# The middle 1024 columns of both mixers' output projections as a pair of column blocks on eight PSUM banks, three of its eight couples by seven products

## The chip, the core and the metric

One NeuronCore of a Trainium2 chip runs the whole program in one launch. TensorE (PE) multiplies into PSUM, eight banks of 512 float32 columns on 128 partitions; VectorE (DVE), ScalarE (ACT) and GpSimd (POOL) do the elementwise work; SyncE (SP) issues the weight transfers. Each engine works through its own queue in order and waits on semaphores of the others. The metric is device time in microseconds, the median of several runs. Before the change it is 2400.95 us (2400.9 to 2401.26, three runs).

## What is computed

The reference is a two-layer encoder trunk on 256 tokens of width 2048, in float32. A layer is a norm, a token mixer with a residual add, a second norm and a gated feed-forward with a residual add. Layer 0 mixes with an mLSTM, layer 1 with an HGRN2; both end in an output projection `y @ w_out`, 256 x 2048 times 2048 x 2048, which is what the change touches.

```python
for layer in range(DEPTH):
    hn = rmsnorm(h, norm_mix_g[layer])
    if layer % N_MIXERS == 0:
        mix = mlstm_mixer(hn, ...)      # ends in  y @ w_out
    else:
        mix = hgrn_mixer(hn, ...)       # ends in  y @ w_out
    h = h + mix
    h = h + conv_glu(rmsnorm(h, norm_ffn_g[layer]), w_up, conv_w, conv_b, w_down)
return rmsnorm(h, final_g)
```

## The kernel before

**Precision.** A float32 product is made of three matmuls in a faster type (`F32R`). Each operand is split into a high part, which is the value rounded to that type, and a low part, which is the rest; then hi x hi, hi x lo and lo x hi are added in PSUM. For weights the split is done while the kernel runs: `parts` (L130) copies 1024 columns of `raw` to `wh` on ACT (L133) and subtracts on DVE, `wl = raw - wh` (L134). Activations are split once, by `split` (L325), into tiles of 128 features whose first 256 columns are the high part of all tokens and whose last 256 are the low part.

**The stream.** The program is a list of `Chunk`s, run by `stream` (L258). Each chunk reads its weights through one common sequence of pieces: `load_raw` (L123) brings 2048 columns into one of three `raw` buffers, and `parts` turns these into pieces of 1024 columns in rings of four `wh` and four `wl` tiles (`WB`). `fetch` keeps `LOOK` = 3 pieces ahead of PE. There are three kinds of chunk. "fm" makes 128 features x 256 tokens with the weights as the stationary operand (L304, L308). "tm" makes 256 tokens x 512 columns in two PSUM banks with the activations as the stationary operand (L320), 16 tiles x 2 token halves x 3 matmuls = 96 matmuls. "st" makes 256 tokens x 1024 columns, a pair of column blocks, in all eight banks (`squares_by_seven`, L204).

**A couple by seven.** In "st" two activation tiles and two column blocks form a couple: with token halves and tiles it is a 2 x 2 block matrix A times a 2 x 2 block matrix B, 8 products of 3 matmuls, 24 matmuls of 128 x 512. For the couples in `ch.seven` a scheme after Strassen and Winograd makes it with 7 products, 21 matmuls. It needs sums of the blocks of B (`combine`, L178: T1 to T4, one of them from `raw` in a 1024-wide subtraction, L184, two in 512-wide ones, L186 and L187, then split into `th` by ACT, L189, and `tl` by DVE, L190) and sums of the blocks of A (`token_sums`, L1003, into a tile `sx` with high and low part). Four of the seven products belong to more than one of the four results. They are gathered in four banks of their own, P1, P6, P7 and P5 (pool `psm`), while the other three go straight to the four result banks C11, C12, C21 and C22 (pool `psa`). After the last couple by seven `mid` (L1021) adds the four shared banks to the residual `hm` through `u2` and `u3`: a copy on ACT, five 512-wide adds on DVE and three on POOL (L1030 to L1032). After the last couple `done` adds the result banks (L1037). Before the change this serves the first parts of the feed-forward's down projection, with `SEVEN` = couples 1, 3, 5 and 7 of eleven.

**Output projections.** Before the change, each mixer's output projection is four "tm" chunks of 512 columns from `project` (L480). When a block is done, two DVE adds put it into `hm` (L486), and `norm.add(c)` (L367) sums its squares on ACT and queues `turn` (L372), which transposes the four new 128-feature tiles on PE through a bank of pool `psa` (L379) and splits them into the next stage's activations `xt` (L326, L327). Side work of that sort waits in the list `side`, which is stepped between matmuls. The next stage's first up run needs all sixteen `xt` tiles.

**Order.** The code names an order, and the framework's list scheduler then reorders instructions within each engine by its own cost estimates, as the program is built; only instructions wrapped in `pin` keep theirs. What is said below about positions in a queue was read from the built programs.

**Names.** `ya` and `yb` are the output projections' activations in the mLSTM and the HGRN. `mm` are tiles of the four `psm` banks, `pc` and `pz` tiles of the four `psa` banks. `LEAD` is an unused tile that shifts what follows it in SBUF. `idle` (L1096) are matmuls on ones that PE makes while the first weights load.

Of the kernel before, what the change touches and what calls it, by code (L numbers as in the profile page):

```python
# [15 lines left out]
P = 128  # L16
T = 256
# [30 lines left out]
SEVEN = (1, 3, 5, 7)  # L48

# [7 lines left out]
def trunk_kernel(ctx, tc, xT, x_d, fg_d, pp_d, cst_d, w_gate, w_first, w_aq, w_ak, w_av, w_ao, w_aout,  # L57
                 w_bq, w_bv, w_bg, w_bout, w_up, w_d0, w_d1, w_d2, out, mscr):
# [53 lines left out]
    side = Side()  # L112
# [56 lines left out]
    def split_squares(ch, parts):  # L169
# [23 lines left out]
        for u in range(units):  # L193
            r = raw(u)
            if u + 1 in ch.seven:
                combine(u + 1)
            wh, wl = parts(r[:, 0:1024], 1024)
            yield wh, wl, 1
            if 2 * u + 1 < ch.nk:
                m = 512 if u in ch.seven else 1024  # L200
                wh, wl = parts(r[:, 1024:1024 + m], m)
                yield wh, wl, sums.pop(u, None)

    def squares_by_seven(ch, fetch, ready):  # L204
# [4 lines left out]
        begun = set()  # L209

# [13 lines left out]
        for u in range(units):  # L224
# [120 lines left out]
    class Norm:  # L345
# [26 lines left out]
        def turn(self, c):  # L372
            yield 2.5
            for k0 in (4 * c, 4 * c + 2):
                pz = aux("pz")
                for k in (k0, k0 + 1):
                    for t in range(2):
                        o = (k - k0) * T + t * P
                        pe.transpose(pz[:, o:o + P], hm[:, t, k * P:(k + 1) * P], ident)  # L379
                for k in (k0, k0 + 1):  # L380
                    self.take(k, pz[:, (k - k0) * T:(k - k0 + 1) * T])
                yield 1.0
            if c == 3:
                self.total()
                self.finish()
                self.spread()
# [108 lines left out]
    def slot(j, name, more=None):  # L495
        where = keep if j < KT else more
        return where.tile([P, 2 * T], F32R, tag=f"yt{j}", name=f"{name}{j}")


    def mlstm(norm, nxt):  # L500
# [273 lines left out]
        def end():  # L774
            side.drain()
            stack.close()

        tail = project(lambda c: w_aout[c], KT, yx, nxt)
        tail[1].before = end
        return chunks + tail  # L780


    def hgrn(norm, nxt):
# [197 lines left out]
        def end():  # L981
            side.drain()
            stack.close()

        tail = project(lambda c: w_bout[c], KT, yx, nxt)
        tail[1].before = end
        return chunks + tail


    def ffn(layer, norm, nxt):  # L990
# [11 lines left out]

        def token_sums(u, a, b, S, SX):  # L1003

            sx = box["mp"].tile([P, 1024], F32R, tag=f"sx{SEVEN.index(u)}", name="sx")
            for i, (x, y, op) in enumerate(((a[:, P:T], b[:, P:T], ALU.add), (a[:, P:T], a[:, 0:P], ALU.subtract),
                                            (S[:, 0:P], a[:, 0:P], ALU.subtract), (b[:, 0:P], S[:, 2 * P:3 * P], ALU.subtract))):
                dve.tensor_tensor(S[:, i * P:(i + 1) * P], x, y, op)
            act.copy(sx[:, 0:512], S)
            dve.tensor_tensor(sx[:, 512:1024], S, sx[:, 0:512].bitcast(F32), ALU.subtract)  # L1010
            SX[u] = sx

        def pair(src, nk, q, GT, SX, norm):

            u = []

            def part(t, c):
                o = 1024 * q + 512 * c
                return hm[:, t, o:o + 512]

            def mid(ps):  # L1021
                P1, P6, P7, P5 = ps
                u2, u3 = (box["mp"].tile([P, 512], F32, tag=n, name=n) for n in ("u2", "u3"))
                act.copy(u2, P1)
                dve.tensor_tensor(part(0, 0), part(0, 0), P1, ALU.add)
                dve.tensor_tensor(u2, u2, P6, ALU.add)
                dve.tensor_tensor(u3, u2, P7, ALU.add)  # L1027
                dve.tensor_tensor(part(1, 1), part(1, 1), P5, ALU.add)
                dve.tensor_tensor(u2, u2, P5, ALU.add)
                pool.tensor_tensor(part(1, 0), part(1, 0), u3, ALU.add)  # L1030
                pool.tensor_tensor(part(1, 1), part(1, 1), u3, ALU.add)
                pool.tensor_tensor(part(0, 1), part(0, 1), u2, ALU.add)  # L1032

            def done(ps):
                for i in range(4):
                    h = part(i // 2, i % 2)
                    dve.tensor_tensor(h, h, ps[i], ALU.add)  # L1037
                if norm is not None:
                    norm.add(2 * q)
                    side.push(second())  # L1040

            def second():
                yield 3.0
                norm.add(2 * q + 1)

            ch = Chunk("st", src, nk, lambda k: GT[k], done)
            ch.mid, ch.seven, ch.sums = mid, SEVEN, lambda u: SX[u]
            pairs.append(ch)
            return ch

        def done_up(f, i, GT, SX):
            def go(ps):
# [15 lines left out]
                if i % 2 and i // 2 in SEVEN:  # L1068
                    token_sums(i // 2, box["c"], c, avc[:, 0:2 * T], SX)
# [3 lines left out]
        for part, (f0, nf) in enumerate(((0, FA), (FA, FB))):  # L1073
            GT, SX = [], {}
            for i in range(nf):
                chunks.append(Chunk("fm", w_up[layer, f0 + i], KT, norm.x, done_up(f0 + i, i, GT, SX),
                                    begin if f0 + i == 0 else None,
                                    swap=(1 + (layer == 0),) if part and i == 0 else ()))
            chunks.append(pair(w_d0[layer][:, f0 * 1024:(f0 + nf) * 1024], nf, 0, GT, SX, nxt if part else None))
# [4 lines left out]
            else:  # L1084
                chunks.append(pair(w_d1[layer], nf, 1, GT, SX, None))
# [8 lines left out]
    for i in range(56):  # L1094
        o = i % 4 * QUAD
        pe.matmul(idle[o:o + QUAD, 0:86], ones[:, 0:QUAD], ones[:, 0:86], start=True, stop=True)  # L1096
# [46 lines left out]
def layout(x, norm_mix_g, norm_ffn_g, mlstm_w_in, mlstm_b_gate, mlstm_head_g, mlstm_w_out, hgrn_w_in, hgrn_lb,  # L1143
# [8 lines left out]
    def squares(q, n):  # L1152

        v = down[:, :n, :, 2 * q:2 * q + 2]
        m = n // 2
        w = v[:, :2 * m].reshape(2, m, 2, P, 2, 512)
        w = np.stack([w[:, :, 0, :, 0], w[:, :, 1, :, 1], w[:, :, 1, :, 0], w[:, :, 0, :, 1]], axis=3)
        w = w.transpose(0, 2, 1, 3, 4).reshape(2, P, m * 2048)
        return np.ascontiguousarray(np.concatenate([w, v[:, 2 * m:].transpose(0, 2, 1, 3, 4).reshape(2, P, -1)], axis=2))

    up = A(ffn_w_up).reshape(2, KT, P, 2, FT, P).transpose(0, 4, 2, 1, 3, 5)
# [14 lines left out]
        w_aout=_cols(A(mlstm_w_out)[0], 512),  # L1176
        w_bq=_cols(qfb, 256),
        w_bv=_cols(wb[:, 2048:4096], 512), w_bg=_cols(wb[:, 4096:6144], 512),
        w_bout=_cols(A(hgrn_w_out)[0], 512),
        w_up=np.ascontiguousarray(up).reshape(2, FT, P, KT * 256),  # L1180
        w_d0=squares(0, FT), w_d1=squares(1, FA),
# [4 lines left out]
def build(nc, ins, out_shape=(2, P, D), **kw):  # L1186
# [4 lines left out]
    with tile.TileContext(nc, schedule_with_timeline_sim=True) as tc:  # L1191
        with ExitStack() as ctx:
            trunk_kernel(ctx, tc, ap["xT"], ap["x"], ap["fg"], ap["pp"], ap["cst"], ap["w_gate"], ap["w_first"],
                         ap["w_aq"], ap["w_ak"], ap["w_av"],
                         ap["w_ao"], ap["w_aout"], ap["w_bq"], ap["w_bv"], ap["w_bg"],
                         ap["w_bout"], ap["w_up"], ap["w_d0"], ap["w_d1"], ap["w_d2"], out, mscr, **kw)
# [12 lines left out]
```

## Time and profile before

| | us |
|---|---|
| median of three runs | 2400.95 |
| the profiled execution | 2402.44 |
| its span in the trace | 2400.6 |
| PE busy | 2388.8 |
| DVE busy | 1829.0 |
| ACT busy | 1260.8 |
| POOL busy | 185.5 |

The granted TensorE clock is 0.999 of full speed over the span. "Busy" adds up instructions of an engine; matmuls are pipelined, so one that lists 390 ns follows another at a smaller distance, which has to be read from the chain or the timeline. A row of a group gives the code line, the engine, output and inputs by name, the shape and count, then busy us and mean ns of one, then the idle time before such instructions and what ended it. The output projection of the mLSTM runs from about 301 to 392 us of the span, that of the HGRN from about 1600 to 1690, and pairs of the feed-forward from 637 to 752, 985 to 1048, 1928 to 2043 and 2280 to 2335.

### The profile page before, as it was taken

To read this page: it belongs to the slowest core of one execution; us is meant where nothing else is said; L and a number is where in the kernel's file an instruction comes from. 1 tells how busy PE (TensorE), PEld (TensorE's weight loads), DVE (VectorE), ACT (ScalarE), POOL (GpSimd) and SP (SyncE) were. 2 spreads that over 40 slices of the span, in tenths; PEclk is the share of its full clock that TensorE was granted. 3 is DMA by queue.
4 is the path that set the end of the run, shared out by engine and by line. 5 is a ranking of instruction groups with operands and counts; after the bars stand their busy time and mean duration, and the time that the engine had idled before them with its cause. 6 is when DMAs were issued, how large, how long until landed. Compare 5 with 4: busy or idle time off the path is not lost.

```text
span 2400.6 us, 37188 instructions
## 1 busy us (share of the span) xinstructions
PE 2388.8 (100%) x14606; PEld 2044.3 (85%) x14606; DVE 1829.0 (76%) x3009; ACT 1260.8 (53%) x1959; POOL 185.5 (8%) x242
## 2 busy tenths in 40 slices
PE   9999999999999999999999999999999999999998
PEld 7888888888888888888888888888888888888887
DVE  7766656777887777867898989885777788777784
ACT  7655455555544455555555555555555454444553
POOL 0100000000000000001222222210000000000000
PEclk9999999999999999999999999999999999999999
DMA  8654555555555555555555455545555555555654
GB/s 299 199 185 163 188 176 180 191 192 193 186 212 198 185 188 190 201 184 180 174 176 173 165 174 176 176 161 191 189 187 189 191 196 208 193 180 189 202 195 147
DMA packets 67679, 451.19 MB, mean 188 GB/s; under 512 B 7712, under 2 KB 8224, under 8 KB 15024
## 3 DMA queue, kind: packets, MB, share of 16 engines
q1 hardware_dynamic: 65520, 444.29, 54.4%
q0 software_dynamic: 1120, 3.21, 0.8%
q8 instruction: 114, 1.87, 0.3%
q10 hardware_dynamic: 864, 1.32, 0.2%
q14 instruction: 61, 0.50, 0.1%
HBM read 446.63 MB, written 2.16 MB: 187 GB/s over the span
## 4 chain that ended last, share of the span: by engine, by line
PE 99%; DMA 0%; issue 0%; ACT 0%; SPq 0%; DVE 0%; POOLq 0%; POOL 0%
PE mm L304 37%; PE mm L320 26%; PE mm L308 18%; PE pc L214 11%; PE mm L214 3%; PE pn L657 1%; PE py L921 1%; PE pd L871 0%; PE pz L379 0%; PE pa L871 0%; DMA raw<-in_w_first 0%; PE S L643 0%; PE pz L942 0%; PE pa L896 0%; PE pa L895 0%; PE pz L685 0%
## 5 line engine op out<-in xcount | busy, mean ns | idle before, releaser
L134 DVE TENSOR_TENSOR wl<-raw,wh 128x1024 fp32r<-128x1024 f32 (+1 forms) x846 | 1016.4, 1207 | 429.0 <-ACT wh L133 420.2
L304 PE MATMUL mm<-xt,wh 128*128 128x512 f32 x3776 | 1318.4, 395 | 0.0
L133 ACT CAST wh<-raw 128x1024 fp32r<-128x1024 f32 (+1 forms) x846 | 861.4, 1028 | 762.4 <-issue 260.2
L308 PE MATMUL mm<-xt,wl 128*128 128x256 f32 x3776 | 1049.2, 279 | 0.0
L304 PEld LDWEIGHTS mm<-xt,wh 128*128 128x128 f32 x3776 | 706.8, 188 | 162.3
L308 PEld LDWEIGHTS mm<-xt,wl 128*128 128x128 f32 x3776 | 710.3, 188 | 4.1 <-issue 0.4
L320 PE MATMUL mm<-wh,xt 128*128 128x512 f32 x1024 | 320.2, 391 | 2.0 <-ACT xt L326 1.1
L320 PEld LDWEIGHTS mm<-wh,xt 128*128 128x128 f32 x1024 | 191.5, 188 | 41.8 <-ACT xt L326 1.5
L214 PE MATMUL pc<-wh,g 128*128 128x512 f32 x704 | 225.2, 389 | 0.0
L320 PE MATMUL mm<-wl,xt 128*128 128x512 f32 x512 | 198.0, 391 | 0.0
L331 ACT COPY b<-mm 128x256 f32<-128x256 f32 x236 | 87.4, 370 | 158.8 <-PE mm L308 158.7
L214 PEld LDWEIGHTS pc<-wh,g 128*128 128x128 f32 x704 | 132.1, 188 | 27.5
L214 PE MATMUL pc<-wl,g 128*128 128x512 f32 x352 | 136.0, 389 | 0.0
L320 PEld LDWEIGHTS mm<-wl,xt 128*128 128x128 f32 x512 | 96.2, 188 | 18.9
L332 DVE TENSOR_TENSOR avc<-mm,b 128x256 f32<-128x256 f32 x172 | 72.0, 420 | 41.4 <-ACT b L331 41.3
L320 PE MATMUL mm<-wh,g 128*128 128x512 f32 x308 | 96.4, 391 | 0.0
L1030 POOL TENSOR_TENSOR hm<-hm,u 128x512 f32<-128x512 f32 x6 | 7.8, 1296 | 1015.5 <-DVE u L1027 1015.5
L320 PE MATMUL mm<-wh,yb 128*128 128x512 f32 x256 | 80.7, 393 | 0.0
L320 PE MATMUL mm<-wh,ya 128*128 128x512 f32 x256 | 80.6, 393 | 0.0
L214 PEld LDWEIGHTS pc<-wl,g 128*128 128x128 f32 x352 | 66.1, 188 | 13.6
L189 ACT CAST th<-T 128x1024 fp32r<-128x1024 f32 x48 | 49.1, 1052 | 48.7 <-DVE T L187 15.5
L337 DVE TENSOR_TENSOR avc<-avc,R 128x256 f32<-128x256 f32 x172 | 72.1, 421 | 2.8
(227 smaller groups left out, 2236.7 us busy)
## 6 DMA issues: line engine op xcount, KB each, us to landing
raw<-in_w_up SPq DMA_DIRECT2D x172, 1024.0 KB, 4.9
raw<-in_w_d SPq DMA_DIRECT2D x84, 1024.0 KB, 4.9
raw<-in_w_bq SPq DMA_DIRECT2D x48, 1024.0 KB, 5.0
raw<-in_w_ao SPq DMA_DIRECT2D x16, 1024.0 KB, 4.8
raw<-in_w_aout SPq DMA_DIRECT2D x16, 1024.0 KB, 4.8
raw<-in_w_bv SPq DMA_DIRECT2D x16, 1024.0 KB, 4.8
raw<-in_w_bg SPq DMA_DIRECT2D x16, 1024.0 KB, 4.8
raw<-in_w_bout SPq DMA_DIRECT2D x16, 1024.0 KB, 4.8
```

The costliest lines, as they stand in the source:

```text
L133: pin(act.copy(wh[:, :m], r))
L134: pin(dve.tensor_tensor(wl[:, :m], r, wh[:, :m].bitcast(F32), ALU.subtract))
L189: act.copy(th[:, c], t)
L214: pe.matmul(ps, a, b, start=id(ps) not in begun, stop=stop and i == 2)
L304: pe.matmul(ps[f], wh[:, c:c + P], x, start=k + kk == 0, stop=False)
L308: pe.matmul(ps[f][:, 0:T], wl[:, c:c + P], x[:, 0:T], start=False, stop=k + kk == ch.nk - 1)
L320: pe.matmul(ps[t], x[:, a + t * P:a + (t + 1) * P], w[:, c], start=st and i == 0, stop=sp and i == 2)
L331: act.copy(b, ps[:, T:2 * T])
L332: dve.tensor_tensor(dst, ps[:, 0:T], b, ALU.add)
L337: dve.tensor_tensor(dst, dst, R, ALU.mult)
L657: pe.matmul(pn[:, 0:258], w, v, start=(i == 0), stop=(i == len(parts) - 1))
L921: pe.matmul(py[:, c], AT[:, s if s == t else 2 + s], V[:, s, j * P:(j + 1) * P], start=(s == 0), stop=(s == 1))
```

## The change

In both mixers the four column blocks become three chunks: block 0 as before ("tm"), then blocks 1 and 2 together as one "st" chunk over sixteen activation tiles, that is eight couples, then block 3 as before. Couples 2, 4 and 6 (`SEVEN_MIX`) are made by seven products, the other five by eight. The weights of blocks 1 and 2 are laid out in couples outside the kernel (`w_ao2`, `w_bo2`).

What comes with it: `combine` for these couples, issued after the first piece of the couple before (`late`) in place of ahead of it; the token sums, which here are made by a side job `token` once block 0 is done, from two 256-wide adds per couple (tile `f`, high plus low part) and `token_sums`; `mid` and `done` for the pair; and a small SBUF pool `op`, opened when block 0 is done and the mixer's own pool has been closed, and closed ahead of block 3. As the pair holds all eight banks, `turn` waits while it runs (`held`), so the transposes of blocks 0, 1 and 2 come during block 3.

`token_sums` and `pair` move out of `ffn` and get more arguments; the feed-forward uses them as before. Two more edits stand in the diff: in layer 1 the first up run of the second part has the order of two matmuls exchanged at the third place, as layer 0 has, and no longer at the second (`swap`), and the idle matmuls at the start are 61 of 79 columns in place of 56 of 86.

```diff
+SEVEN_MIX = (2, 4, 6)
@@ split_squares
         for u in range(units):
             r = raw(u)
-            if u + 1 in ch.seven:
+            if u + 1 in ch.seven and not ch.late:
                 combine(u + 1)
             wh, wl = parts(r[:, 0:1024], 1024)
             yield wh, wl, 1
+            if u + 1 in ch.seven and ch.late:
+                combine(u + 1)
@@ squares_by_seven
         begun = set()
+        held.append(ch)
...
+        held.pop()
         ch.done(psa_)
@@ Norm.turn
             yield 2.5
+            while held:
+                yield 1.0
@@ token_sums and pair, moved out of ffn
+    def pair(src, nk, c0, x, sums, norm, seven, late=False):
+        def part(t, c):
+            o = 512 * (c0 + c)
+            return hm[:, t, o:o + 512]
+        def mid(ps):
+            P1, P6, P7, P5 = ps
+            u2, u3 = (ch.pool.tile([P, 512], F32, tag=n, name=n) for n in ("u2", "u3"))
+            act.copy(u2, P1)
+            dve.tensor_tensor(part(0, 0), part(0, 0), P1, ALU.add)
+            dve.tensor_tensor(u2, u2, P6, ALU.add)
+            dve.tensor_tensor(u3, u2, P7, ALU.add)
+            dve.tensor_tensor(part(1, 1), part(1, 1), P5, ALU.add)
+            dve.tensor_tensor(u2, u2, P5, ALU.add)
+            pool.tensor_tensor(part(1, 0), part(1, 0), u3, ALU.add)
+            pool.tensor_tensor(part(1, 1), part(1, 1), u3, ALU.add)
+            pool.tensor_tensor(part(0, 1), part(0, 1), u2, ALU.add)
+        def done(ps):
+            for i in range(4):
+                h = part(i // 2, i % 2)
+                dve.tensor_tensor(h, h, ps[i], ALU.add)
+            if norm is not None:
+                norm.add(c0)
+                side.push(second())
...
+    def mixed(w, w2, x, norm, close):
+        c0, _, _, c3 = project(lambda c: w[c // 3], KT, x, norm)
+        op, SX, first = ExitStack(), {}, c0.done
+        def sums(u):
+            side.until(lambda: u in SX)
+            return SX[u]
+        two = pair(w2, KT, 1, x, sums, norm, SEVEN_MIX, True)
+        def token():
+            for i, u in enumerate(SEVEN_MIX):
+                f = two.pool.tile([P, 1024], F32, tag="avc", bufs=2, name="f")
+                for j in range(2):
+                    y = x(2 * u + j).bitcast(F32)
+                    dve.tensor_tensor(f[:, j * T:(j + 1) * T], y[:, 0:T], y[:, T:2 * T], ALU.add)
+                SX[u] = token_sums(two.pool, i, f[:, 0:T], f[:, T:2 * T], f[:, 2 * T:4 * T])
+                yield 5.0
+        def done(ps):
+            side.drain()
+            close()
+            two.pool = op.enter_context(tc.tile_pool(name="op", bufs=1))
+            two.pool.tile([P, LEAD], F32, name="lead")
+            first(ps)
+            side.push(token())
+        c0.done, c3.before = done, op.close
+        return [c0, two, c3]
@@ mlstm (hgrn the same, with w_bout and w_bo2)
-        tail = project(lambda c: w_aout[c], KT, yx, nxt)
-        tail[1].before = end
-        return chunks + tail
+        return chunks + mixed(w_aout, w_ao2, yx, nxt, stack.close)
@@ ffn
-                                    swap=(1 + (layer == 0),) if part and i == 0 else ()))
+                                    swap=(2,) if part and i == 0 else ()))
@@ start
-    for i in range(56):
+    for i in range(61):
         o = i % 4 * QUAD
-        pe.matmul(idle[o:o + QUAD, 0:86], ones[:, 0:QUAD], ones[:, 0:86], start=True, stop=True)
+        pe.matmul(idle[o:o + QUAD, 0:79], ones[:, 0:QUAD], ones[:, 0:79], start=True, stop=True)
```

More of the change, by code (lines that the diff above doesn't have):

```diff
@@ L1001, in begin @@
                 nxt.begin(box["mp"])
[L1003 to L1049, printed above, removed]
         def done_up(f, i, GT, SX):
@@ L1084, in ffn @@
             else:
[L1085 removed]
+                chunks.append(two(w_d1[layer], 2, None))
         return chunks, stack.close
```

63 lines of the change are left out of this document (37 added, 26 removed).

## The prediction

> **What bounds the kernel now.** I read the page's head first, then the chain that ended last, then PE's waits, to see whether PE work or a wait sets the end.
>
> ```profile
> span 2400.6 us, 37188 instructions
> PE 2388.8 (100%) x14606; PEld 2044.3 (85%) x14606; DVE 1829.0 (76%) x3009; ACT 1260.8 (53%) x1959; POOL 185.5 (8%) x242
> PE 99%; DMA 0%; issue 0%; ACT 0%; SPq 0%; DVE 0%; POOLq 0%; POOL 0%
> ```
> ```profile
> PE idle L1096 <- POOL ones L1089: 1.1, 1, 1.1
> PE mm L320 <- ACT xt L326: 1.1, 1, 1.1
> PE mm L320 <- ACT wh L133: 0.9, 1, 0.9
> ```
>
> TensorE (PE) is 99% of the chain, and all its waits together are 3.1 us, each seen once, in the start. So a matmul that goes away gives its full spacing, unless a wait appears that was not there. The spacing is read from runs of 128x512 matmuls in the chain (start, length, count):
>
> ```profile
> 375.56 16.35 PE mm L320 x72
> 637.44 5.47 PE pc L214 x24
> 677.59 18.36 PE pc L214 x81
> ```
>
> 18.36 / 81 is 0.2267 us and 16.35 / 72 is 0.2271 us. The 0.39 us that groups of matmuls list is the length of one, most of it under the next; the price is 0.2267.
>
> **The room on the other engines.** The stage that changes is the output projection of a mixer. The first row below is the last three of its four column blocks in the mLSTM; the other two are pairs of the feed-forward, which already work as the change will (four couples of eleven by seven products). Columns: stretch, its length, busy PE, PEld, DVE, ACT, POOL.
>
> ```profile
> 323.40:391.90 68.50, 68.50 (x315) 56.76 (x315) 38.63 (x44) 33.77 (x48) 0.00 (x0) 1.00 0.55 186
> 637.44:694.65 57.21, 57.21 (x253) 47.33 (x253) 50.80 (x59) 30.02 (x36) 3.80 (x3) 1.00 0.57 198
> 694.65:752.00 57.35, 57.35 (x255) 47.48 (x253) 46.01 (x50) 26.68 (x30) 3.80 (x3) 1.00 0.60 209
> ```
>
> DVE is at 56% in the projection and at 89% in the first feed-forward pair, and PE waits in neither. The durations that price the change:
>
> ```profile
> L134 DVE TENSOR_TENSOR wl<-raw,wh 128x1024 fp32r<-128x1024 f32 (+1 forms) x846 | 1016.4, 1207 | 429.0 <-ACT wh L133 420.2
> L133 ACT CAST wh<-raw 128x1024 fp32r<-128x1024 f32 (+1 forms) x846 | 861.4, 1028 | 762.4 <-issue 260.2 <-PE mm L320 204.0 <-PE mm L304 181.3
> L190 DVE TENSOR_TENSOR tl<-T,th 128x1024 fp32r<-128x1024 f32 x48 | 57.4, 1219 | 4.2 <-ACT th L189 4.2
> L189 ACT CAST th<-T 128x1024 fp32r<-128x1024 f32 x48 | 49.1, 1052 | 48.7 <-DVE T L187 15.5 <-PE pc L214 13.4 <-issue 12.8
> L1063 DVE TENSOR_TENSOR avc<-avc 128x256 f32<-128x256 f32 x86 | 35.8, 416 | 1.0 <-ACT avc L1062 1.0
> L184 DVE TENSOR_TENSOR T<-raw 128x1024 f32<-128x1024 f32 x24 | 29.3, 1219 | 3.8 <-DMA raw<-in_w_d 3.7
> L327 DVE SCALAR_TENSOR_TENSOR xt<-pz,pp,xt 128x256 fp32r<-128x256 f32 x48 | 21.8, 479 | 8.6 <-ACT xt L326 8.4
> L1008 DVE TENSOR_TENSOR avc<-avc 128x128 f32<-128x128 f32 x64 | 18.4, 287 | 1.1
> L186 DVE TENSOR_TENSOR T<-raw,T 128x512 f32<-128x512 f32 x24 | 16.5, 690 | 0.6
> L1037 DVE TENSOR_TENSOR hm<-hm,pc 128x512 f32<-128x512 f32 x24 | 15.5, 679 | 1.6 <-PE pc L214 1.6
> L1010 DVE TENSOR_TENSOR sx<-avc,sx 128x512 fp32r<-128x512 f32 x16 | 10.9, 684 | 0.0
> L1009 ACT CAST sx<-avc 128x512 fp32r<-128x512 f32 x16 | 9.8, 615 | 0.0
> ```
>
> In a full queue they come closer together. From the timeline, with the three adds that POOL makes after a pair's last couple by seven:
>
> ```profile
> 644.00 3.49 DVE L134 TENSOR_TENSOR wl<-raw,wh 128x1024 fp32r<-128x1024 f32 x3
> 750.00 1.28 DVE L1037 TENSOR_TENSOR hm<-hm,pc 128x512 f32<-128x512 f32 x2 [0.33 <-PE pc L214]
> 738.35 0.69 DVE L1029 TENSOR_TENSOR u<-u,mm 128x512 f32<-128x512 f32 x1
> 741.27 3.29 DVE L134 TENSOR_TENSOR wl<-raw,wh 128x1024 fp32r<-128x1024 f32 x2 [2.23 <-ACT wh L133]
> ```
> ```profile
> 738.55 1.30 POOL L1030 TENSOR_TENSOR hm<-hm,u 128x512 f32<-128x512 f32 x1 [53.33 <-DVE u L1027]
> 739.80 1.29 POOL L1031 TENSOR_TENSOR hm<-hm,u 128x512 f32<-128x512 f32 x1
> 741.05 1.29 POOL L1032 TENSOR_TENSOR hm<-hm,u 128x512 f32<-128x512 f32 x1
> ```
>
> A 1024-wide subtraction takes 3.49 / 3 = 1.16 us of queue, a 512-wide add 1.28 - 0.68 = 0.60. The two subtractions at 741.27 take 3.29 in place of some 2.33: 0.96 more, and the last POOL add runs until 742.34, 1.07 after their start. The first one stood still while POOL added.
>
> **The change, part by part.**
>
> *Products (gain).* A couple by seven has 7 products of 3 matmuls where it had 8. Three couples in each of two mixers: 18 matmuls fewer, 18 x 0.2267 = 4.08 us. The rest of the middle 1024 columns keeps its count, and so does the number of transposes: the 24 of the first three blocks move behind the pair (the `held` list) into the last block's matmuls. The tiles they make are first read by the feed-forward, at least 12 us later, so the move is free unless they wait for a bank (below).
>
> *DVE, ACT and POOL per mixer (cost hidden or not).* Added on DVE: three `combine`, each 1.219 + 0.690 + 0.690 + 2 x 1.219 = 5.04, less the half split that is no longer needed (1.207 - 0.69 = 0.52); three token sums, each 2 x 0.416 + 4 x 0.287 + 0.684 = 2.66; five 512-wide adds in `mid`, 3.4. Sum 3 x (5.04 - 0.52 + 2.66) + 3.4 = 24.9. On ACT 6 x 1.052 + 3 x 0.615 and one 512-wide copy, about 8.8, less 3 x 0.4. On POOL 3 x 1.29. DVE would then hold 38.63 + 24.9 = 63.5 us of the 66.5 that are left of the three blocks, 96%, by stand-alone durations; some of that can start in the block before (the built order has the first `combine` there).
>
> *Does DVE keep up?* I went through the built order of each engine. From the end of the first block to the end of the pair DVE has 18 instructions of 1024, 14 of 512, 6 of 256 and 12 of 128 columns: 18 x 1.16 + 14 x 0.60 + 6 x 0.416 + 12 x 0.287 = 35.2 us, at stand-alone durations 37.4, while PE has 183 matmuls, 41.5 us. It fits, so what counts is the order. Three places are tight:
>
> 1. mLSTM, couple 4 (from 0): the second `tl` half. DVE cannot split the couple's first piece before PE has left that buffer, 24 matmuls into couple 2. Then come the cast, 1.03, and on DVE four 1024-wide (the `tl` half is the last), three 512-wide, two 256-wide and four 128-wide: 4 x 1.16 + 3 x 0.60 + 2 x 0.416 + 4 x 0.287 = 8.4 us, 8.9 at stand-alone durations. PE's first use is 44 matmuls, 10.0 us, after the release: 0.1 to 0.6 ahead.
> 2. HGRN, couple 2: the cast of the first piece stands on ACT behind a cast of the last piece of couple 1 and the token-sum cast. From the release by block 0's last matmul: 1.028 + 0.615 + 1.028 = 2.7 us, and PE is there 11 matmuls, 2.5 us, later: 0.2 late, or on time if the casts overlap a little, as wide ones on DVE do.
> 3. After the HGRN pair: from P6's last matmul PE has 22 matmuls, 5.0 us, until it reads the last block's third piece; DVE has u2, one `xt`, u3, u2 and that split, 0.68 + 0.48 + 0.68 + 0.69 + 1.16 = 3.7 us. 1.3 to spare. In the mLSTM 32 matmuls and four transposes lie there, 7.3 us or more.
>
> A late split delays what stands behind it on DVE, and PE behind that. I take 0.2 us for place 2 and nothing for the others; the ends are 0, since the feed-forward pairs run this scheme at 89% DVE without a PE wait, and 1.0, if each place is late by a semaphore's 0.2 to 0.5.
>
> *Weight DMA.* The same 457 issues on SP, the same bytes. A buffer comes free later, since `combine` reads a couple early and the split late.
>
> ```profile
> raw<-in_w_bout SPq DMA_DIRECT2D x16, 1024.0 KB, 4.8
> ```
>
> In the HGRN the buffer for couple 4 comes free with the last split of couple 1. Before it on DVE stand two 512-wide adds that wait for block 0's last matmul (29 matmuls, 6.6 us, into the pair) and two 256-wide: 1.2 + 0.83 + 1.16 = 3.2 us; with 4.8 us to land, `combine`'s first instruction and the split of couple 3 behind it (2 x 1.16) this ends at 6.6 + 3.2 + 4.8 + 2.3 = 16.9, and PE needs it after 79 matmuls, 17.9. Price 0; a landing 2 us longer would cost 1.
>
> *Idle matmuls.* 56 x 86 columns become 61 x 79, 4816 against 4819: the same length.
>
> ```profile
> 1.10 3.63 PE L1096 MATMUL idle<-ones 128*32 128x86 f32 x112 [1.10 <-POOL ones L1089]
> 5.63 1.19 PE L320 MATMUL mm<-wh,xt 128*128 128x512 f32 x4 [0.91 <-ACT wh L133]
> 6.67 0.62 PE L320 MATMUL mm<-wl,xt 128*128 128x512 f32 x2
> ```
>
> The first real matmul waits 0.9 us for a cast that they do not touch. What they could change is the pace behind them: the first four matmuls take 1.04 us (5.63 to 6.67) where full pace takes 0.91. Price 0, with 0.13 either way, and 0.4 if the matmuls after the start's other wait (1.1 us) change with them. *The swap* in layer 1's first up run of the second part exchanges two neighbouring matmuls: 0, with 0.2 at most either way.
>
> **The sum.** -4.08 + 0.2 = -3.9 us. The profiled execution took 2402.44 us (span 2400.6), 1.5 over the median of the runs, 2400.95. It would become 2398.5, and the median 2397.1, with 2396.3 to 2398.4 from the ends above. That is -0.16%. A measurement of this kernel can tell about 0.2%, 4.8 us, from no change, so this counts as "same": 18 matmuls are worth less than the threshold even if nothing is lost.
>
> **The rivals.**
>
> *POOL shuts DVE out (2399.0).* In a feed-forward pair DVE has nothing to do during POOL's first two adds, because it waits for ACT; only the third costs 0.96. In a mixer the last couple by seven is the last but one, so DVE's queue is full then. If DVE's two-input work stands still from the first add to the end of the third, 3 x 1.27 = 3.8 us, then at place 3 u3 is done 1.8 us after P6, POOL ends at 5.8, and the split at 6.9 against 5.0: 1.9 late in the HGRN, nothing in the mLSTM (7.3 us and an earlier start). -3.9 + 1.9 = -2.0. For it speaks the row at 741.27; against it that POOL, too, may have to wait between DVE's instructions, and then the hm adds wait instead. The Trainium skill, SBUF — State Buffer, "Who interferes with whom", says that a DVE instruction with two SBUF inputs and a GpSimd instruction that reads SBUF exclude each other for a whole instruction, whoever starts first. By that rule the trace agrees for one add (0.96 us); for three in a row no run here shows it, and the time by it is that of this rival.
>
> *The gain turns into waits (2401.2).* 96% DVE by stand-alone durations could mean that PE simply follows DVE in the pair: each mixer gives back its 2.04. Price +4.1 against the gain. For it: the sum of 63.5 in 66.5. Against: 35.2 in 41.5 within the pair.
>
> *Slower (2409).* DVE is late at every couple by seven: T, `th`, `tl` and the token sum of one couple hang on single buffers that PE must leave first, so lateness does not recover between couples. At 2 us for each of six couples it is +12 - 4.1 = +7.9, 2408.9. It decides against the change from 1.5 us a couple, (4.08 + 4.8) / 6. For it: place 1 has 0.1 us to spare by the upper sum. Against: the feed-forward has the same chain at every second couple, with DVE at 89%, and PE never waits.
>
> *More gain (2396.0).* The start wins 0.7 us or more by the other idle matmuls and no wait comes: -4.08 - 0.8 = -4.9. Nothing in the rows of the start asks for more than 0.4.
>
> **How the numbers follow.** Forecast (2396.3 to 2398.4) 0.50; POOL 0.17; gain lost to waits 0.15; slower 0.10; more gain 0.08. The forecast, POOL and the lost gain all lie within 0.2%: 0.82 same. Faster by over 0.2% needs 2396.1 or less, 0.08; slower 0.10. The range from 2396.2 to 2401.6 holds the three middle cases, 0.82; the likeliest's own is 2396.3 to 2398.4.
>
> **What would show it.** Right: PE's instructions fall by 18 matmuls (its records by 18, plus 10 for the idle ones); PE's waits stay at three in the start and short ones inside the mixers' pairs; the blocks of a mixer from its first output matmul to the feed-forward's are 2.0 us shorter; DVE is near 90% there. Wrong: a PE wait on DVE `wl` after the HGRN pair (POOL), on `tl` or `sx` at couples 2, 4, 6 (DVE behind), or on a bank that an hm add has not read yet; or a start that differs by more than 0.5 us.

## The result and the profile after

The changed kernel takes 2397.69 us, the kernel before 2401.30 in the same comparison (medians of 20 runs each): 3.61 us less, a ratio of 0.9985 with a 95% interval of 0.9978 to 0.9992. The forecast was 2397.1. The total is near, but the runs below show that it is a sum of four terms, two of which, of 4.5 us each and of opposite sign, the forecast did not have.

The page's head and the chain of the changed kernel:

```profile
span 2395.9 us, 37279 instructions
PE 2385.3 (100%) x14598; PEld 2042.5 (85%) x14598; DVE 1872.3 (78%) x3091; ACT 1272.1 (53%) x1979; POOL 197.4 (8%) x248
PE 97%; DVE 1%; DMA 1%; issue 0%; ACT 0%; POOL 0%; POOLq 0%; DVEq 0%; ACTq 0%
```

PE's waits in it:

```profile
PE idle L1124 <- POOL ones L1117: 1.1, 1, 1.1
PE mm L325 <- ACT xt L331: 0.6, 1, 0.6
PE pn L741 <- DVE Wl L733: 0.2, 1, 0.2
```

PE's records fall by 8, from 14606 to 14598, as 18 matmuls less and 10 records of idle matmuls more (five matmuls, two records each) make it. No wait inside the projections is listed. The three blocks from the end of block 0 on, in the mLSTM and in the HGRN (columns as in the prediction; behind POOL stand the granted clock, the DMA share and GB/s):

```profile
320.91:389.03 68.12, 68.12 (x314) 56.48 (x313) 60.74 (x85) 40.49 (x59) 5.78 (x3) 1.00 0.57 191
1609.50:1678.09 68.59, 68.47 (x314) 56.41 (x312) 60.95 (x86) 40.55 (x60) 5.78 (x3) 1.00 0.55 190
```

DVE goes from 38.6 to 60.7 us there, 89%, with 22 us added where 24.9 were estimated. In the mLSTM's pair alone it is at 39.80 of 41.63 us, 96%:

```profile
323.37:365.00 41.63, 41.63 (x185) 34.48 (x185) 39.80 (x58) 23.50 (x31) 0.30 (x1) 1.00 0.58 199
```

To see where the time went, I read from PE's timeline when marked matmuls start: the first and the last that reads `ya`, the first of the first down pair of each layer, the first and the last that reads `yb`, and PE's last. An up run is a stretch of the feed-forward's up projection; each layer has two. The stretches between them, in us, and the time of each kernel (beside it the median of before in its comparison):

| kernel | to `ya` | mLSTM projection | layer 0, first up run | to `yb` | HGRN projection | layer 1, first up run | rest | time (before) |
|---|---|---|---|---|---|---|---|---|
| before | 300.96 | 90.57 | 245.75 | 950.68 | 94.79 | 245.75 | 462.99 | 2401.30 |
| changed | 300.47 | 88.55 | 245.71 | 950.11 | 93.24 | 250.25 | 458.53 | 2397.69 (2401.30) |
| all by eight | 299.64 | 90.59 | 250.25 | 950.12 | 94.81 | 250.25 | 458.53 | 2406.22 (2401.51) |
| both old small edits | 300.48 | 88.55 | 245.71 | 951.19 | 93.87 | 250.25 | 462.99 | 2403.56 (2401.51) |
| mLSTM only | 300.18 | 88.55 | 245.71 | 950.73 | 94.79 | 245.75 | 458.53 | 2395.32 (2401.51) |
| sums' copy on POOL | 299.98 | 88.60 | 245.72 | 950.77 | 92.76 | 250.25 | 458.53 | 2398.09 (2401.51) |
| old swap | 300.22 | 88.55 | 245.71 | 950.73 | 93.24 | 250.25 | 462.99 | 2401.94 (2401.18) |
| exchange, third place | 300.14 | 88.55 | 245.71 | 950.11 | 93.22 | 245.71 | 458.53 | 2393.00 (2401.18) |
| exchange, second place | 299.96 | 88.55 | 245.71 | 950.13 | 93.22 | 245.70 | 458.53 | 2392.89 (2401.18) |
| swap alone | 299.74 | 90.57 | 245.75 | 950.35 | 94.79 | 245.75 | 458.53 | 2396.57 (2401.18) |
| exchange + copy on POOL | 300.37 | 88.60 | 245.72 | 950.73 | 92.76 | 245.70 | 458.53 | 2393.69 (2401.47) |
| POOL loaded | 300.22 | 89.11 | 245.71 | 950.74 | 101.81 | 245.70 | 458.53 | 2402.38 (2401.47) |
| four by seven | 300.14 | 92.25 | 245.75 | 950.57 | 100.96 | 250.19 | 458.53 | 2409.32 (2401.47) |
| five by seven | 300.05 | 100.79 | 250.25 | 951.40 | 104.23 | 245.70 | 458.53 | 2422.03 (2401.47) |

The projections became 2.02 and 1.55 us shorter, which is the change. But layer 1's first up run, whose matmuls nobody touched, became 4.50 longer, and the rest, which holds layer 1's second up run, 4.46 shorter. -2.02 - 0.04 - 1.55 + 4.50 - 4.46 = -3.57, against -3.61 between the medians. The first and fourth columns scatter from kernel to kernel with no order in them (299.64 to 300.96, 950.11 to 951.40); the profiled execution of before stands at the upper end of the first.

The up runs' two lengths show as two paces. Three equal stretches of 200 us in three up runs (layer 0's first, layer 1's first and second), before:

```profile
400.00:600.00 200.00, 200.00 (x1157) 175.00 (x1156) 152.20 (x255) 102.35 (x150) 0.00 (x0) 1.00 0.57 190
1700.00:1900.00 200.00, 200.00 (x1156) 174.83 (x1155) 153.59 (x257) 102.43 (x150) 0.00 (x0) 1.00 0.58 191
2060.00:2260.00 200.00, 200.00 (x1134) 173.34 (x1133) 148.98 (x248) 99.16 (x146) 0.00 (x0) 1.00 0.56 186
```

and after:

```profile
400.00:600.00 200.00, 200.00 (x1156) 175.01 (x1155) 152.54 (x255) 102.05 (x150) 0.00 (x0) 1.00 0.57 189
1700.00:1900.00 200.00, 200.00 (x1134) 173.41 (x1133) 151.05 (x253) 99.24 (x147) 0.00 (x0) 1.00 0.56 187
2060.00:2260.00 200.00, 200.00 (x1156) 174.86 (x1156) 152.35 (x254) 101.12 (x149) 0.00 (x0) 1.00 0.57 190
```

PE is 100% busy at a granted clock of 1.00 in all six, and does 1156 matmuls in some and 1134 in others, 1.9% fewer. A pair of a 512-wide matmul with `wh` and a 256-wide one with `wl` takes 0.347 us at one pace and 0.353 at the other (0.3467 and 0.3533 between starts); a layer's first up run has 704 pairs, its second 672. Before, the last run had the slower pace; after, the last but one.

### The profile page after: what moved, and what is told of

The parts are those of the page before. It is cut to its first block, busy times and chain, and to the rows that moved or that the text cites. A ratio compares the mean times of both kernels' runs of the same rounds, so it can differ in the third digit from the quotient of the medians.

```text
span 2395.9 us, 37279 instructions
## 1 busy us (share of the span) xinstructions
PE 2385.3 (100%) x14598; PEld 2042.5 (85%) x14598; DVE 1872.3 (78%) x3091; ACT 1272.1 (53%) x1979; POOL 197.4 (8%) x248
## 4 chain that ended last, share of the span: by engine, by line
PE 97%; DVE 1%; DMA 1%; issue 0%; ACT 0%; POOL 0%; POOLq 0%; DVEq 0%; ACTq 0%
PE mm L309 36%; PE mm L325 22%; PE mm L313 18%; PE pc L218 14%; PE mm L218 3%; PE pn L741 1%; PE py L999 1%; PE pd L949 0%; PE pz L386 0%; PE pa L949 0%; DVE wl L135 0%; DMA Mb<-mscr 0%; DMA raw<-in_w_first 0%; PE S L727 0%; PE pz L1020 0%
## 5 line engine op out<-in xcount | busy, mean ns | idle before, releaser
L190 ACT CAST th<-T 128x1024 fp32r<-128x1024 f32 x60 | 61.8, 1052 | 55.3 <-DVE T L188 18.4
L191 DVE TENSOR_TENSOR tl<-T,th 128x1024 fp32r<-128x1024 f32 x60 | 72.1, 1221 | 4.1 <-ACT th L190 4.0
L941 DVE COPY kq<-QK 128x256 f32<-128x256 f32 x224 | 69.9, 337 | 0.0
```

Source lines behind the costliest of these rows:

```text
L190: act.copy(th[:, c], t)
L191: dve.tensor_tensor(tl[:, c], t, th[:, c].bitcast(F32), ALU.subtract)
L941: dve.tensor_copy(m[:, j].rearrange("k (m p j) -> k m p j", p=2, j=h), blocks(z, h, 0, T))
```

## Experiments

### The pair on eight banks without products by seven

```diff
-SEVEN_MIX = (2, 4, 6)
+SEVEN_MIX = ()
@@ squares_by_seven: no shared banks where ch.seven is empty
```

> The pair stays on eight banks with the transposes held, but all eight couples by eight products: nothing of combine, token sums and mid in the mixers. Theory (the gain is the 18 matmuls, less a wait of 0.3 us and a slow pace of 0.1 behind it at the HGRN's couple 2): 18 x 0.2267 - 0.39 = 3.7 us above the changed kernel's 2397.7, so 2401.4, the time before; each mixer's blocks as long as before. Rival (the arrangement on eight banks has a gain or a loss of its own): more than 0.5 us away from 2401.4.

2406.22 against 2401.51, +4.71. The theory's total fails, and the rival's condition is met in letter, but not by the projections: they take 90.59 and 94.81 us, as before to 0.02. So in the projections the arrangement itself is worth nothing, and the products are worth 2.0 us a mixer. What is above 2401.4 is in the up runs: both layers' first are longer than before and layer 1's second is shorter, +4.50 + 4.50 - 4.46 = +4.54.

### The two small edits undone

```diff
-    for i in range(61):                         # idle matmuls 128x79
+    for i in range(56):                         # 128x86
-        swap=(2,) if part and i == 0 else ()
+        swap=(1 + (layer == 0),) if part and i == 0 else ()
```

> The changed kernel with the idle matmuls (56 x 86) and the swap of before. Theory (both small edits cost and bring nothing beyond a run's own scatter): 2397.7, within 0.3. Rival (the changed start brings what the profile shows, PE 0.66 us ahead at 62 us and 0.48 ahead at 82 us): 2398.2, with the waits on a cast of wh (0.9) and on xt (1.1) back.

2403.56, 5.9 above the changed kernel; neither theory had that. The rest is back at 462.99, so 4.46 are the last up run. Its waits, further, name two that the changed kernel does not have, of 0.4 us each, at 1416 and 1595 us, in two stretches that are 1.08 and 0.63 longer than in the changed kernel:

```profile
PE mm L309 <- issue: 0.4, 1, 0.4
PE pd L949 <- issue: 0.4, 1, 0.4
```

### The HGRN's projection as before

```diff
@@ hgrn
-        return chunks + mixed(w_bout, w_bo2, yx, nxt, stack.close)
+        ...                                     # end(): drains `side`, closes the mixer's pool
+        tail = project(lambda c: w_bout[c], KT, yx, nxt)
+        tail[1].before = end
+        return chunks + tail
```

> The mLSTM's projection as changed, the HGRN's as before. Theory (each mixer gives its 9 matmuls, 2.04, less its own waits, none in the mLSTM and 0.39 in the HGRN): 2401.3 - 2.04 = 2399.3, that is 1.65 above the changed kernel. Rival (the whole gain is the mLSTM's or the start's, the HGRN gives nothing): 2397.7. Rival (DVE is behind in the mLSTM and the gain is the HGRN's): 2401.

2395.32, 6.19 below before and 2.4 below the changed kernel, outside all three. The mLSTM's projection keeps its 88.55 and the HGRN's is back at 94.79, as the theory has it; but layer 1's first up run is at 245.75 again. Undoing half of the gain brought a faster up run with it.

### The copy of the token sums off ACT

```diff
@@ token_sums
-    def token_sums(mp, i, a, b, S):
+    def token_sums(mp, i, a, b, S, copy=act.copy):
...
-        act.copy(sx[:, 0:512], S)
+        copy(sx[:, 0:512], S)
@@ token
-                SX[u] = token_sums(two.pool, i, f[:, 0:T], f[:, T:2 * T], f[:, 2 * T:4 * T])
+                SX[u] = token_sums(two.pool, i, f[:, 0:T], f[:, T:2 * T], f[:, 2 * T:4 * T],
+                                   act.copy if i else pool.tensor_copy)      # i = 0: couple 2
```

> The changed kernel, but the high part of the token sums of couple 2 is copied by POOL and not by ACT, in both mixers. Theory (the HGRN's couple 2 waits because the cast of its first piece stands on ACT behind this copy, 0.6 us): the wait of 0.28 at that place and the slow pace behind it go, 0.39 in all, 2397.3. Rival (the cast is late because block 0's last matmul releases its buffer late, whatever stands on ACT): the wait stays, 2397.7. Rival (POOL's copy is slower than ACT's and shuts DVE out, so that the low part of the sums comes late): a longer wait at couple 2, 2398 or more.

In the changed kernel the place looks like this, PE first (start, length, count), then ACT:

```profile
1618.15 1.52 PE L218 MATMUL pc<-wh,yb 128*128 128x512 f32 x6
1619.79 0.50 PE L218 MATMUL mm<-wh,yb 128*128 128x512 f32 x1
1620.13 0.39 PE L218 MATMUL mm<-th,sx 128*128 128x512 f32 x1
```
```profile
1617.21 1.05 ACT L134 CAST wh<-raw 128x1024 fp32r<-128x1024 f32 x1 [1.55 <-PE mm L325]
1618.17 0.61 ACT L513 CAST sx<-f 128x512 fp32r<-128x512 f32 x1
1618.69 1.05 ACT L134 CAST wh<-raw 128x1024 fp32r<-128x1024 f32 x1
```

Six matmuls from 1618.15 would let the next start at 1619.51; it starts at 1619.79, 0.28 late, just behind the cast that ends at 1619.74, and the next one 0.34 after it in place of 0.23. With the copy on POOL:

```profile
1618.36 1.52 PE L218 MATMUL pc<-wh,yb 128*128 128x512 f32 x6
1619.72 0.39 PE L218 MATMUL mm<-wh,yb 128*128 128x512 f32 x1
1619.94 0.39 PE L218 MATMUL mm<-th,sx 128*128 128x512 f32 x1
```
```profile
1617.67 0.61 POOL L513 CAST sx<-f 128x512 fp32r<-128x512 f32 x1 [13.02 <-DVE f L512]
```

The gap is gone and the HGRN's projection takes 92.76, 2.03 less than before: the whole of its nine matmuls. That the cast stood behind the copy is shown, and the two rivals fall. The time, 2398.09, is not lower than 2397.69; the stretch to `yb` was 950.77 here and 950.11 there.

After these four the theory that the gain is the matmuls less one wait held for the projections and failed for the time. The new theory: an up run goes at one of two paces, set by the order of PE's matmuls at its start.

### The swap alone, from both sides

```diff
@@ the changed kernel, idle matmuls as changed
-        swap=(2,) if part and i == 0 else ()
+        swap=(1 + (layer == 0),) if part and i == 0 else ()
```

> The changed kernel with the swap of before in layer 1's second up run, the idle matmuls as changed. Theory (an up run goes at one of two paces, 0.347 or 0.353 us for a pair of a 512- and a 256-wide matmul, set by the order at its start; the swap's place sets it for the last run, 704 pairs): +704 x 0.0063 = 4.4, so 2402.1, and 0.353 in the windows from 2060 to 2260 us. Rival (the idle matmuls made the 5.9 us of the run with both old edits, or part of them): 2397.7 to 2400.

2401.94: as expected within 0.2, though the last run has 672 pairs and not 704; 672 x 0.0066 is 4.4. The three stretches of this kernel:

```profile
400.00:600.00 200.00, 200.00 (x1155) 174.86 (x1154) 152.63 (x255) 102.00 (x149) 0.00 (x0) 1.00 0.56 189
1700.00:1900.00 200.00, 200.00 (x1134) 173.52 (x1133) 150.87 (x253) 99.67 (x147) 0.00 (x0) 1.00 0.56 187
2060.00:2260.00 200.00, 200.00 (x1134) 173.40 (x1133) 148.86 (x247) 99.44 (x146) 0.00 (x0) 1.00 0.55 186
```

The new projections without the swap are thus no faster than the kernel before (+0.76; ratio 1.0003, 0.9994 to 1.0012): their 3.57 us go to layer 1's first up run behind them, 4.50.

```diff
@@ the kernel before
-        swap=(1 + (layer == 0),) if part and i == 0 else ()
+        swap=(2,) if part and i == 0 else ()
```

> The kernel before with only the swap moved from the second to the third place in layer 1's second up run. Theory (the swap alone sets the pace of the last up run): 2401.5 - 4.4 = 2397.1, with 0.347 from 2060 to 2260 us; the whole change would then bring nothing over this one edit. Rival (the last run's pace comes with the new projections, and the swap does nothing without them): 2401.5.

2396.57, 4.61 below before (0.9981, 0.9972 to 0.9990), with 458.53 in the rest and nothing else changed. One exchange of two neighbouring matmuls does more than the whole change.

### An exchange for the run that became slow

```diff
-        swap=(2,) if part and i == 0 else ()
+        swap=(2,) if i == 0 and (part or layer) else ()
@@ and the other one
+        swap=(2,) if part and i == 0 else (1,) if layer and i == 0 else ()
```

> The changed kernel with two neighbouring matmuls exchanged at the third place of layer 1's first up run too (1680 to 1928 us), which goes at 0.353. Theory (the pace is set by the order at the run's start): if this place sets the faster pace, 704 x 0.0063 = 4.4 less, 2393.3; if not, 2397.7 with 0.353 there. Rival (the slower pace there is made by the work on the other engines or by the clock, not by PE's order): 2397.7 at every place.

> As the run before, with the exchange at the second place. Theory (pace set by the order at the start): one of the two places gives 2393.3, or both; a place that does not gives 2397.7. Rival (another engine's work makes the pace): 2397.7 in both.

2393.00 and 2392.89, both places work: layer 1's first up run takes 245.7 us, with one pair of neighbouring matmuls exchanged and PE's order otherwise the same. Its stretches, with the exchange at the second place:

```profile
1700.00:1900.00 200.00, 200.00 (x1156) 174.83 (x1155) 152.94 (x256) 100.75 (x149) 0.00 (x0) 1.00 0.56 190
2060.00:2260.00 200.00, 200.00 (x1156) 174.83 (x1155) 152.58 (x255) 101.14 (x149) 0.00 (x0) 1.00 0.57 191
```

DVE and ACT get slightly more done per stretch, since they follow PE. So one pair of PE's matmuls can switch the pace with the work of the other engines and the clock as they were; the rival, 2397.7 at every place, falls.

That the order alone sets the pace does not follow, and the traces speak against it. By tile and shape, the 1420 matmuls between the last one that reads `yb` and layer 1's first down pair come in one and the same order in eight kernels. Three of them go at the faster pace (before, swap alone, mLSTM only) and five at the slower one (changed, all by eight, both old small edits, sums' copy on POOL, old swap). All by eight, to be held against the row of before above:

```profile
1700.00:1900.00 200.00, 200.00 (x1135) 173.44 (x1134) 150.61 (x252) 101.10 (x148) 0.00 (x0) 1.00 0.56 185
```

These two begin alike: the first nine pairs of the run take 3.17 us before (1682.97 to 1686.14) and 3.18 in all by eight (1685.62 to 1688.80), the slower pace in both. Only behind the transposes and the four `pr` matmuls that interrupt the run in its first 10 us does before go over to the faster pace, and all by eight does not. What decides there is open.

The exchange at the second place makes the fastest kernel of the study, 8.3 us below before, a ratio of 0.9965 (0.9952 to 0.9979), and 4.8 below the change as it was made.

> The run with the exchange at the second place of layer 1's first up run (2392.9), and POOL in place of ACT copying the high part of couple 2's token sums. Theory (the two add up; the copy on POOL takes the wait of 0.28 at the HGRN's couple 2 away and the slow matmul behind it, 0.39 in all): 2392.5, and the HGRN's stage 2.0 us shorter than before in place of 1.6. Rival (what is won at the couple comes back in the pace of a later stretch): 2392.9 or more.

This one joins the two edits shown above. 2393.69: the HGRN's projection gets its 92.76, yet the time is not lower. The stretch to `yb` was 0.6 longer than in the run at 2392.89, as in the other run with the copy on POOL; whether the copy does that or chance is open, since the old swap's kernel has the longer stretch too and differs from the changed one only behind it. The time is where the rival put it, but no later stretch has lost its pace.

### POOL loaded

```diff
@@ token, once for each of the three couples
+                for _ in range(3):
+                    pool.tensor_tensor(z, z, z, ALU.add)        # 128x512
```

> As the run at 2392.9, with nine more 512-wide adds on POOL in each mixer's pair (on a tile z that nothing else reads). Theory (POOL and DVE take turns, so an add costs DVE some 0.4 to 0.5 us, as at the pair's end, where three adds cost it 1.1 to 1.5): 9 x 0.45 = 4 us in a pair that leaves DVE some 6, so 2392.9 to 2394. Rival (DVE's two-input work stands still while POOL adds): 9 x 1.27 = 11.4 us, 5 over the room in each pair, 2393 + 10 = 2403.

2402.38, near the rival's 2403, but by luck: the rival had each pair 5 us late, and the mLSTM lost 0.56 and the HGRN 8.6. In the mLSTM the adds ran mostly ahead of the pair. In the HGRN they ran beside its first couples; DVE's rows there, then POOL's (first a single add of the mLSTM with no two-input split beside it, then the HGRN's nine, then the last of these alone), then PE's waits:

```profile
1611.55 2.06 DVE L135 TENSOR_TENSOR wl<-raw,wh 128x1024 fp32r<-128x1024 f32 x1
1614.98 2.06 DVE L191 TENSOR_TENSOR tl<-T,th 128x1024 fp32r<-128x1024 f32 x1
1616.96 1.52 DVE L188 TENSOR_TENSOR T<-raw,T 128x512 f32<-128x512 f32 x1
```
```profile
312.68 1.04 POOL L573 TENSOR_TENSOR z<-z 128x512 f32<-128x512 f32 x1
1611.13 14.04 POOL L573 TENSOR_TENSOR z<-z 128x512 f32<-128x512 f32 x9
1623.07 2.10 POOL L573 TENSOR_TENSOR z<-z 128x512 f32<-128x512 f32 x1
```
```profile
PE mm L218 <- ACT wh L134: 5.2, 1, 5.2
PE pc L218 <- ACT wh L134: 0.9, 1, 0.9
```

DVE is not shut out for the whole chain of adds: it goes on, at 2.06 us for a split that takes 1.22 and 1.52 for a sum that takes 0.68, 0.84 more for each. POOL is slowed as well, 14.04 / 9 = 1.56 an add, up to 2.10, where the single one takes 1.04. From the split at 1611.55 to the start of the second `tl` split, 1623.06, DVE took 11.5 us, where the changed kernel takes 5.3 for the same instructions (1610.62 to 1615.89): 6.2 us late. Eight adds were over by then, so an add cost 0.8, where I had 0.45. PE waits at the very place of the HGRN's couple 2, through the chain DVE sums, ACT copy, ACT cast. And the wait has a price of its own, seen in the windows:

```profile
1621.30:1627.00 5.70, 0.50 (x4) 0.06 (x2) 5.67 (x9) 1.65 (x3) 3.71 (x3) 0.84 0.00 0
1628.00:1629.00 1.00, 1.00 (x4) 0.81 (x3) 1.00 (x3) 0.68 (x3) 0.00 (x0) 0.50 0.00 0
1632.00:1633.00 1.00, 1.00 (x6) 0.82 (x5) 0.00 (x0) 0.00 (x0) 0.00 (x0) 1.00 1.03 344
```

Behind it the granted clock is 0.50 and matmuls stand 0.427 us apart in place of 0.227, for some 5 us, which costs 2.5. With the waits of 5.2 and 0.9 that is the HGRN's 8.6.

### A fourth and a fifth couple

```diff
-SEVEN_MIX = (2, 4, 6)
+SEVEN_MIX = (2, 4, 5, 6)          # and (2, 3, 4, 5, 6); th and tl with two buffers
```

> As the run at 2392.9, with couples 2, 4, 5 and 6 by seven products, th and tl in two buffers each and three buffers of token sums. Six matmuls fewer, 1.36 us; on DVE 6.2 us more in each pair, 41.4 in all against 40.8 of PE. Theory (DVE's room in the pair is used up by the fourth couple): each pair late by 0.6 us or more, so 2392.7 to 2396. Rival (the neighbouring blocks take DVE's surplus): 2391.5.

> As the run before, with couples 2 to 6 by seven. Twelve matmuls fewer than at 2392.9, 2.7 us; DVE 47.6 us in each pair against 40.1 of PE. Theory (PE follows DVE): 7.5 us late in each pair less what the blocks beside it take, 2398 to 2405. Rival (the neighbouring blocks take the surplus, PE waits for nothing): 2390.2.

2409.32 and 2422.03: DVE's room is used up by the third couple, and my prices for going over it were too low. The six runs with four couples go from 2404.1 to 2412.1, wider than those of any other kernel here, and only the one at 2409.43 has a trace. With four, in that run:

```profile
PE mm L325 <- ACT wh L134: 3.5, 3, 1.9
PE pc L218 <- DVE wl L135: 2.1, 2, 1.3
PE mm L218 <- DVE tl L191: 1.4, 3, 0.6
```
```profile
1656.50:1657.50 1.00, 1.00 (x4) 0.82 (x5) 1.00 (x1) 1.00 (x2) 0.00 (x0) 0.50 0.04 16
1660.00:1662.30 2.30, 2.30 (x7) 1.77 (x6) 1.43 (x3) 0.32 (x1) 0.00 (x0) 0.50 0.00 0
```

The projections take 3.7 and 7.7 us more than with three, of which some 3 are the half clock (half of the 6.1 us from 1656.5 to 1662.6 in the HGRN), and layer 1's first up run falls to its slower pace again, 250.19, although it has the exchange that cured it: 3.7 + 7.7 + 4.5 = 15.9 of the 16.4 above 2392.89. That run's row:

```profile
1700.00:1900.00 200.00, 200.00 (x1135) 173.62 (x1134) 150.61 (x252) 100.38 (x147) 0.00 (x0) 1.00 0.56 187
```

The run's 1420 matmuls stand in the same order as with the exchange at the second place, where 1156 are done in this window. With five the two projections take 12.2 and 11.0 more, layer 1's first up run is fast in that same order, and it is layer 0's first up run that is slow, in an order that goes at the faster pace in ten other kernels.

## Why the prediction was right, and where not

*Products, -4.08.* Right: with eight products in all couples the projections are as long as before, with seven 2.02 shorter in the mLSTM and, without the wait, 2.03 in the HGRN, nine times 0.2267.

*Place 2, 0.2 late.* Right in place and mechanism, 0.28 measured, with 0.2 more behind it: 2.03 - 1.55 = 0.48 in all, where 0.2 stood in the sum. The range's 1.0, a semaphore's 0.2 to 0.5 at every place, did not come: at this place PE starts 0.05 us behind the end of the cast. *Place 1* is looser than I had it. The second `tl` half, then PE's first use:

```profile
346.46 1.22 DVE L191 TENSOR_TENSOR tl<-T,th 128x1024 fp32r<-128x1024 f32 x1
```
```profile
349.50 0.39 PE L218 MATMUL mm<-tl,sx 128*128 128x512 f32 x1
```

It is 1.8 us ahead, not 0.1 to 0.6. *Place 3* is tighter, 0.6 in place of 1.3, because of POOL:

```profile
1657.59 1.92 DVE L135 TENSOR_TENSOR wl<-raw,wh 128x1024 fp32r<-128x1024 f32 x1
1660.42 1.32 DVE L135 TENSOR_TENSOR wl<-raw,wh 128x1024 fp32r<-128x1024 f32 x1
```
```profile
1657.12 1.30 POOL L532 TENSOR_TENSOR hm<-hm,u 128x512 f32<-128x512 f32 x1 [52.68 <-PE pc L218]
1658.38 2.28 POOL L533 TENSOR_TENSOR hm<-hm,u 128x512 f32<-128x512 f32 x1
1660.63 2.27 POOL L534 TENSOR_TENSOR hm<-hm,u 128x512 f32<-128x512 f32 x1
```

The split ends at 1659.51 and PE needs it at 1660.10. *The POOL rival* is wrong here: DVE is not held for all three adds, the second and third add wait for DVE instead. (Its sum, 1.8 + 3.8, is 5.6 and not 5.8, too.) The nine adds show that such turns can make DVE late all the same. *The gain turns into waits* and *slower* did not come, but the fourth couple shows how near they were.

*The swap, "0, with 0.2 at most either way".* This step failed. It is worth -4.46, more than the products; the kernel before with this edit alone takes 4.61 less. I priced an exchange of neighbours by the work it adds. It is the last run's 672 pairs at 0.347 in place of 0.353 us. The rows for another price were in the profile of before: 1157 and 1156 matmuls in 200 us of two up runs, 1134 in the third, at the same clock and with no wait. I asked only where PE waits, and a PE that is 100% busy at a lower pace has no wait.

*The move of the transposes, "free unless they wait for a bank".* The step stopped at waits as well. With the changed projection ahead of it, layer 1's first up run goes at the slower pace, +4.50. The run's own matmuls stand in the order of before, so the cause comes from ahead of it or from the moment at which its interruptions fall. Which of the two, and whether the moved transposes have a part in it, is not settled: the arrangement without products by seven has the slower pace too, and in layer 0 as well, where the changed kernel does not. The place of the tiles in SBUF, which the new pool may shift, was not varied alone either.

*Idle matmuls, 0.* Not wrong at the start, where the first matmuls scatter with both versions alike (62 us into the span PE was between 1.3 and 0.5 us ahead of before in all runs, new and old idle matmuls). The changed kernel's 0.66 is over the 0.5 that I had named as a sign of being wrong, but the swap alone, with the old idle matmuls, is 1.2 ahead. The two kernels that differ in them alone take 2403.56 and 2401.94, however, in two comparisons whose kernel before differs by 0.3, and the slower one has the two waits on issue, 0.4 each, far behind. I can't say what makes them.

So 2397.1 came out near 2397.7 since two terms that I did not have, -4.46 and +4.50, cancel. That is luck. The range would have been missed with either of them alone: 2393 or 2402.

## What to carry to other kernels

Before pricing an edit on a saturated engine, count its instructions per equal stretch wherever the same loop runs: two counts at the same clock mean a pace that an edit can switch, and that no list of waits shows. The edit need not stand in that loop. After a change, compare stretches nobody touched; a total alone may hide two errors. Here an engine at 96% beside the bound one was used up, and lateness cost more than itself once the clock dropped.

## What the runs showed of the hardware

- The alternation of a 512-wide and a 256-wide matmul, each with a new 128x128 stationary tile, has two steady paces here, 0.347 and 0.353 us a pair, at a granted clock of 1.00. In the four kernels made for it, exchanging two neighbours at the start of a run moved it from one to the other (4.5 us in 704 or 672 pairs), and from some 20 us on every run kept its pace to its end. The order does not decide alone, since one order went at either pace in different kernels. What does I can't tell.
- Two-input work on DVE and adds on POOL slow each other: on DVE 1.22 becomes 2.06 and 0.68 becomes 1.52, on POOL an add into `hm` goes from 1.30 to 2.28 us and one on `z` from 1.04 to 2.10, in turns. The Trainium skill, SBUF — State Buffer, "Who interferes with whom", has the two exclude each other for a whole instruction. The trace agrees, in the rows of place 3: the first split ends 1.09 us behind the end of the first add (1659.51, 1658.42), the second add 1.15 behind that split (1660.66), the second split 1.08 behind that add (1661.74), and the third add 1.16 behind that split (1662.90). It excludes one instruction at a time: a DVE queue beside a chain of POOL adds gets through all the same.
- A wait of 5.2 us (POOL loaded), and also one of 1.9 with others of up to 1.3 ahead of it (four couples), is followed by 5 to 6 us at a granted clock of 0.50, matmuls at 0.427 us. The Trainium skill, TensorE: Matmul & The Clock Gate, "Part 1: The HAM clock gate", gives the same two clocks and a window of about 3.4 us of idleness; the trace agrees on the clocks. With POOL loaded it agrees on the window too: a mean clock of 0.84 from 1621.3 to 1627.0 means 1.8 us at half, so the drop came at 1625.2, 3.4 us into the wait, which began at 1621.8. With four couples, after waits of 1.9 us and less, the half clock comes earlier than that.
- A cast of 512 columns takes 0.61 us on POOL, as on ACT.
